# Scale and shift of the second layer's experts summed in chunks on VectorE, ScalarE and GpSimd, with the partitions added by TensorE

## The chip, the cores and the metric

One core of a Trainium2 chip. The metric is device time of one execution in microseconds (us), the median over runs; the profile is of one execution. TensorE is the matrix engine, VectorE (DVE), ScalarE (ACT) and GpSimd (POOL) the elementwise engines, SyncE (SP) issues most DMA loads. Each engine takes its instructions in a fixed order and waits on semaphores for what others produce.

## The reference, cut to what matters

A two-layer backbone over 256 latent tokens with 256 context tokens, width 1024, float32. Every sub-layer is modulated: a conditioning vector is multiplied by a 1024 x 6144 matrix per layer, which gives six vectors of 1024: shift, scale and gate of the mixer, shift, scale and gate of the expert layer.

```python
s_lat = jax.nn.silu(c)            # conditioning of the latents
s_ctx = jax.nn.silu(c_ctx)        # conditioning of the context
for layer in range(DEPTH):
    m  = [z[:, None, :] for z in ada_mod(s_lat, ada_w[layer], ada_b[layer])]
    mc = ada_mod(s_ctx, ada_w[layer], ada_b[layer])
    ...
    h = h + m[2] * y                                       # y: the mixer
    f = modulate(rmsnorm(h, norm_ffn_g[layer]), m[3], m[4])
    ...
```

`ada_mod` is `s @ w + b` split in six, `modulate(h, shift, scale)` is `h * (1 + scale) + shift`. In the second (last) layer the context no longer passes through the experts, so there `m[3]` and `m[4]` are needed for the latents only. The second layer's mixer is pooling in four groups beside windowed attention with eight heads of queries, then the output projection `odd_w_out`; the experts are 16 with two chosen per token.

## The kernel before, in words

The kernel runs the layers as phases in one program; in each, a scheduler lays the instructions of every engine into one fixed order. All weights pass as 1-MB tiles of shape [128, 4, 512] through `Stream`, a ring of seven buffers that SyncE fills (L147): a tile's buffer takes the next load when its last reader is done. For the projections, `Stream._prep` splits a half tile into two pieces, `whi` by a ScalarE copy (L176) and `wlo` by a subtraction on VectorE or, every third, on GpSimd (L180).

The modulation is made by `ada(l, i, half)` for half a vector (512 columns): two tiles, eight chunks [128, 512], and for each chunk a matmul (L446) of 32 columns of the conditioning `sT` with the chunk as moving operand, into one of four strips of 32 partitions of a PSUM bank. The strips hold latents and context of up to eight half vectors. `finish` copies the bank to the SBUF tile `part` on ScalarE (L476), adds the partitions with four matmuls on the 0/1 matrix `sel` (L482) and adds the bias on VectorE into `mcol` (L484); `gain` (L472) turns a scale into (1 + scale) times the norm's weight. `finish` puts its second part into `pend`, which `flush` runs later. `part` has two buffers.

The change lies in the second layer's mixer phase, from some 635 to 735 us. It loops over eight attention units (two blocks of queries, four pairs of heads). `scores` makes the scores of a unit on TensorE (L1499), masks them and takes the maximum on VectorE (L1503, L1504), forms the negative maximum `nm` (L1507, L1508), the exponential with its sum on ScalarE (L1515), and normalises `p` on VectorE (L1519). `attend` transposes `p` on TensorE (L1532), copies it to `pTT` on VectorE and ScalarE (L1534) and multiplies by the values (L1539). The scores of the next unit are requested ahead of the products of this one. In the first four rounds a pooling group is done as well (L1479 to L1486, split in L523, L524) and one half vector of modulation, `ada(*next(ada_it))`: the four half vectors of shift and scale for the experts. They share one PSUM bank and have one `finish`. In round 4 `flush` ends them; the rows are written to DRAM and read back spread over the partitions (`rows`, `spread`: L494 to L500, tiles `mrow` and `s4b`). Rounds 4 and 5 hold the output projection (`mix`, products L518 to L520; L528 multiplies by the gate `m2b` into `am`, L529 adds to the stream `H`, on VectorE for one half and on GpSimd for the other). Round 6 and the end prepare the input of the experts, then comes the router and the expert layer, which is matmuls of TensorE against streamed weights to the end.

Of the kernel before, what the change touches and what calls it, by code (L numbers as in the profile page):

```python
# [10 lines left out]
F32 = mybir.dt.float32  # L11
F32R = mybir.dt.float32r
I32 = mybir.dt.int32
AF = mybir.ActivationFunctionType
OP = mybir.AluOpType
# [51 lines left out]
UMAX = 6  # L67
# [145 lines left out]
def backbone(ctx: ExitStack, tc: tile.TileContext, I, out):  # L213
    nc = tc.nc
    V, S, G, T, Q = nc.vector, nc.scalar, nc.gpsimd, nc.tensor, nc.sync
# [3 lines left out]
    sm = ctx.enter_context(tc.tile_pool(name="sm", bufs=2))  # L219
# [13 lines left out]
    def tr_t():  # L233
        return psum.tile([128, 512], F32, name="tr", tag="tr", bufs=2)


    st = Stream(tc, ring, RING, NPIECE)
# [143 lines left out]
    one = cst[:, C_ONE:C_ONE + 128]  # L381
# [18 lines left out]
    c1 = cp.tile([128, 128], F32, name="c1")  # L400
# [18 lines left out]
    pend = []  # L419
    marks = {}  # L420

    def flush():
        while pend:
            pend.pop(0)()
# [11 lines left out]
    def ada(l, i, half, bank=y_t):  # L436

        g, u = group[l, i, half]
        first, last = (l, i, half) == g[0], (l, i, half) == g[-1]
        if first:  # L440
            mods[g] = bank()
        pa = mods[g]
        for s in range(2):
            t = st.take(("ada", l, i, half))
            for j in range(4):
                T.matmul(pa[32 * j:32 * j + 32, :], s_at(s * 4 + j, u), t[:, j, :],  # L446
                         start=first and s == 0, stop=last and s == 1, skip_group_check=True)
            st.done()
        if last:
            l, i, half = min(g)  # L450
            k0 = i * 8 + half * 4
            finish(l, mods.pop(g), len(g), 4, lambda t: t[:, k0:k0 + 4 * len(g)].rearrange("p (u q) c -> p u q c", q=4))
            for i in (1, 4):
                if (l, i, 0) in g:
                    pend.append(lambda i=i: gain(l, i, 0, 8))

    def ada_quarter(q):
        pa = y_t()
# [10 lines left out]
    def gain(l, i, k, n):  # L469
        m = mcol[l][:, i * 8 + k:i * 8 + k + n]  # L470
        gc = c1[:, 96 + 8 * l:104 + 8 * l] if i == 1 else c2[:, 8 * l:8 * l + 8]
        V.scalar_tensor_tensor(m, m, 1.0, gc[:, k:k + n, None].to_broadcast([128, n, 2]), op0=OP.add, op1=OP.mult)  # L472
# [878 lines left out]
    with phase("odd") as op:  # L1351
# [226 lines left out]
        for n, u in enumerate(units):  # L1578
            if n + 1 < len(units):
                scores(*units[n + 1])  # L1580
            if n < 4:
                f = pool_group(n)
            attend(*u)
            if n < 4:
                f()
            if n < 6 - NPRE:
                ada(*next(ada_it))
            if n == 4:
                flush()
                rows(1, 3, 5, 1)  # L1590
                t = op.tile([128, 2, D], F32, name="s4b", tag="band")
                sb["s4"], sb["b3"] = t[:, 0], t[:, 1]
                spread(t[:, 0], 1, 4, 0)
                spread(t[:, 1], 1, 3, 0)
                rws, lgb = router_setup(1, op, 1, rw)
            if n in (4, 5):
                w = st.take(("oo", n - 4))
                for c in range(2):
                    mix(0, c, n - 4, w)
                st.half()  # L1600
                st.done()
            if n == 5:
                ws = [st.take(("ooa", half)) for half in range(2)]
                io = st.taken - 2
                for half in range(2):
                    mix(1, 0, half, ws[half])
            if n == 6:
                ffn_in(0)
                for p in ADA_ODD[6:]:
                    ada(*p, mm_t)  # L1610
# [266 lines left out]
```

## Time and profile before

| | |
|---|---|
| median of 3 runs | 987.55 us (985.78 to 989.07) |
| profiled execution | 986.68 us |
| its span | 984.9 us, mean granted clock of TensorE 0.968 |
| GpSimd busy | 324.9 us |
| ScalarE busy | 313.6 us |
| moved by DMA | 296.27 MB |

The span runs from the first to the last instruction, and the 1.8 us between it and the execution's time lie around it. Busy times are of the engine's own instructions, waits not counted. In a timeline, a row is a run of like instructions on one engine: start, length, line, output and inputs, how many, and in brackets how long the engine stood idle before and which instruction ended that. A matmul in float32 appears as two records, so the four matmuls of L482 read x8.

### The profile page before, as it was taken

What the parts mean: (1) busy time and instruction counts of PE and PEld (TensorE: products, weight loads), DVE (VectorE), ACT (ScalarE), POOL (GpSimd) and SP (SyncE); (2) the same over time, 40 slices, a digit from 0 to 9 for tenths busy, and PEclk for the clock granted to TensorE, in tenths of its full rate; (3) what the DMA queues carried; (4) which work ended last, traced back from release to release, by engine and by line L of the source; (5) the groups of instructions that cost most, each with busy time, mean ns of one, the idle gap of its engine ahead of it and who ended that gap; (6) DMA issues with size and microseconds to landing.
All of it is one profiled execution on the core that took longest, in us unless ns stands there. A gap on an engine that the chain in (4) does not pass through costs nothing. (4 is left out here: it accounts for less than half of the span.)

```text
span 984.9 us, 12562 instructions
## 1 busy us (share of the span) xinstructions
PE 911.3 (93%) x4614; PEld 562.6 (57%) x4614; DVE 501.5 (51%) x903; ACT 313.6 (32%) x460; POOL 324.9 (33%) x231
## 2 busy tenths in 40 slices
PE   3999999988899999999999978898969999999984
PEld 1677667755684668656855647646554444443321
DVE  3562435276783668557774578356652133232222
ACT  3421113033473347226552444244311010010001
POOL 2351103334553465724660544113200022222222
PEclk9999999998899999999999989989979899999998
DMA  9974569848779879789979976259798999999993
GB/s 314 362 259 163 214 216 338 325 142 293 280 267 364 311 268 378 277 322 367 319 262 388 377 248 224 78 150 312 253 368 338 360 371 416 388 362 418 415 396 132
DMA packets 118867, 296.27 MB, mean 301 GB/s; under 512 B 6920, under 2 KB 17176, under 8 KB 110600
## 3 DMA queue, kind: packets, MB, share of 16 engines
q1 hardware_dynamic: 112776, 278.06, 77.2%
q0 software_dynamic: 5984, 17.26, 4.9%
q8 instruction: 40, 0.66, 0.3%
q14 instruction: 35, 0.29, 0.1%
q10 hardware_dynamic: 32, 0.01, 0.0%
HBM read 295.45 MB, written 4.24 MB: 304 GB/s over the span
## 5 line engine op out<-in xcount | busy, mean ns | idle before, releaser
L176 ACT ACTIVATE whi<-w 128x1024 fp32r<-128x1024 f32 x162 | 169.9, 1058 | 183.8 <-PE mm L520 83.3
L180 POOL TENSOR_TENSOR wlo<-w,whi 128x1024 fp32r<-128x1024 f32 x57 | 146.0, 2563 | 224.6 <-ACT whi L176 186.9
L180 DVE TENSOR_TENSOR wlo<-w,whi 128x1024 fp32r<-128x1024 f32 x105 | 157.4, 1512 | 81.8 <-ACT whi L176 81.3
L934 PE MATMUL mm<-w,xh 128*64 128x512 f32 (+2 forms) x680 | 171.4, 602 | 1.2 <-DMA w<-in_moe_w_up_dram 1.2
L529 POOL TENSOR_TENSOR H<-H,am 128x512 f32<-128x512 f32 x64 | 88.8, 1405 | 174.3 <-DVE am L528 171.9
L934 PEld LDWEIGHTS mm<-w,xh 128*64 128x64 f32 (+2 forms) x680 | 53.3, 138 | 94.3 <-issue 87.8
L518 PE MATMUL mm<-whi,xh 128*128 128x512 f32 x160 | 65.9, 412 | 0.8 <-ACT xh L523 0.8
L519 PE MATMUL mm<-wlo,xh 128*128 128x512 f32 x160 | 65.2, 407 | 0.3 <-POOL wlo L180 0.3
L520 PE MATMUL mm<-whi,xl 128*128 128x512 f32 x160 | 64.9, 406 | 0.0
L528 DVE TENSOR_TENSOR am<-mm,m5b 128x512 f32<-128x512 f32 x64 | 42.9, 684 | 27.9 <-PE mm L1262 19.5
L1262 PE MATMUL mm<-y,seT 128*128 128x512 f32 x208 | 54.5, 397 | 0.2 <-ACT y L523 0.2
L519 PE MATMUL mm<-aTl,whi 128*128 128x512 f32 x128 | 51.6, 403 | 2.0 <-POOL aTl L680 2.0
L518 PE MATMUL mm<-aTh,whi 128*128 128x512 f32 x128 | 51.4, 407 | 1.0 <-ACT aTh L679 1.0
L520 PE MATMUL mm<-aTh,wlo 128*128 128x512 f32 x128 | 51.1, 400 | 0.0
L1262 PEld LDWEIGHTS mm<-y,seT 128*128 128x128 f32 x208 | 38.1, 188 | 15.5 <-issue 4.9
L968 PE MATMUL yp<-w,hh 128*64 128x512 f32 (+1 forms) x176 | 42.8, 596 | 0.0
L524 DVE TENSOR_TENSOR yl<-yp,yh 128x512 fp32r<-128x512 f32 x14 | 9.7, 692 | 61.4 <-ACT yh L523 61.4
L446 PE MATMUL yp<-w,sT 128*32 128x512 f32 x288 | 40.8, 625 | 0.0
L934 PE MATMUL yp<-w,hh 128*64 128x512 f32 (+1 forms) x160 | 34.4, 643 | 5.5 <-SPq L1131 3.5
L1053 ACT ACTIVATE sg<-mm 128x512 f32<-128x512 f32 x21 | 12.4, 589 | 82.6 <-PE mm L934 77.1
L518 PEld LDWEIGHTS mm<-whi,xh 128*128 128x128 f32 x160 | 31.2, 195 | 10.9 <-issue 2.7
L1054 DVE SCALAR_TENSOR_TENSOR sg<-sg,slw,mm 128x512 f32<-128x512 f32 x21 | 15.6, 742 | 42.8 <-PE mm L934 42.8
(358 smaller groups left out, 1531.1 us busy)
## 6 DMA issues: line engine op xcount, KB each, us to landing
w<-in_moe_w_gate_dram SPq DMA_DIRECT2D x54, 1024.0 KB
w<-in_moe_w_down_dram SPq DMA_DIRECT2D x54, 1024.0 KB
w<-in_moe_w_up_dram SPq DMA_DIRECT2D x50, 1024.0 KB
w<-in_ada_w_dram SPq DMA_DIRECT2D x48, 1024.0 KB
w<-in_even_w_in_dram SPq DMA_DIRECT2D x8, 1024.0 KB
w<-in_moe_w_gate_dram SPq DMA_DIRECT2D x16, 512.0 KB
w<-in_moe_w_up_dram SPq DMA_DIRECT2D x16, 512.0 KB
w<-in_moe_w_down_dram SPq DMA_DIRECT2D x12, 512.0 KB
```

Source lines behind the costliest of these rows:

```text
L176: self.nc.scalar.activation(hi, t, AF.Copy)
L180: eng.tensor_sub(lo, t, hi.bitcast(F32))
L446: T.matmul(pa[32 * j:32 * j + 32, :], s_at(s * 4 + j, u), t[:, j, :], start=first and s == 0, stop=last and s == 1, skip_group_check=True)
L518: T.matmul(o, lh, rh, start=first, stop=False)
L519: T.matmul(o, lh, rl, start=False, stop=False)
L520: T.matmul(o, ll, rh, start=False, stop=last)
L528: V.tensor_mul(t, pp, m)
L529: eng.tensor_add(acc, acc, t)
L934: T.matmul(o[hs], xh[:, kk, hs].bitcast(F32), w[h][:, k], start=first and k == 0, stop=last and k == 3, skip_group_check=True)
L968: T.matmul(o[hs], hh[:, j, hs].bitcast(F32), w[h][:, k], start=j == 0, stop=j == 3, skip_group_check=True)
L1054: V.scalar_tensor_tensor(sg, sg, w, pu, op0=OP.mult, op1=OP.mult)
L1262: marks["comb"] = T.matmul(pp, seT[n][:, c * 128:(c + 1) * 128], t[:, hs], start=(i == 0), stop=(i == 2 * len(ns) - 1))
```

## The change

For the four half vectors, `ada` is replaced by `ada_sum`, which leaves out the context. It does not multiply on TensorE. The chunk's 128 rows are scaled by the conditioning, one value per partition, and the eight chunks of a half vector are added into two [128, 512] accumulators. Odd chunks go to VectorE: a scaled copy, then three multiply-adds. Even chunks go to ScalarE, a scaled copy into the accumulator, then three scaled copies into a tile `as` that GpSimd adds. The second part, `fin`, adds the 128 partitions: eight matmuls with a 128x128 piece of an accumulator as the weights and a column of ones as the moving operand. Then come the bias and, after the last, the gain. Every `ada_sum` begins with `flush`, so it first emits the `fin` of the one before. The accumulators are the two buffers of `part`; `as` is one of the three buffers `t2k`. Lines of the changed kernel from L489 on are 33 higher than before.

```diff
--- before.py
+++ after.py
@@ -453,6 +453,39 @@
             for i in (1, 4):
                 if (l, i, 0) in g:
                     pend.append(lambda i=i: gain(l, i, 0, 8))
+
+    def ada_sum(l, i, half, tmp):
+
+        flush()
+        accs = [sm.tile([128, 512], F32, name="part", tag="part", bufs=2) for _ in range(2)]
+        for s in range(2):
+            t = st.take(("ada", l, i, half))
+            for j in range(4):
+                a, x = accs[j % 2], sT[:, s * 4 + j, 2 * UMAX - 2:2 * UMAX - 1]
+                if s == 0 and j == 1:
+                    V.tensor_scalar(a, t[:, j, :], x, None, op0=OP.mult)
+                elif j % 2:
+                    V.scalar_tensor_tensor(a, t[:, j, :], x, a, op0=OP.mult, op1=OP.add)
+                elif s == 0 and j == 0:
+                    S.activation(a, t[:, j, :], AF.Copy, scale=x)
+                else:
+                    y = tmp("as")
+                    S.activation(y, t[:, j, :], AF.Copy, scale=x)
+                    G.tensor_add(a, a, y)
+            st.done()
+        k0 = i * 8 + half * 4
+
+        def fin():
+            pc = tr_t()
+            for q in range(4):
+                for n, a in enumerate(accs):
+                    T.matmul(pc[:, q:q + 1], a[:, q * 128:(q + 1) * 128], one[:, 0:1], start=(n == 0), stop=(n == 1))
+            V.tensor_add(mcol[l][:, k0:k0 + 4, 0], pc[:, 0:4], c1[:, 48 * l + k0:48 * l + k0 + 4])
+            if half and i == 4:
+                m = mcol[l][:, i * 8:i * 8 + 8, 0]
+                V.scalar_tensor_tensor(m, m, 1.0, c2[:, 8 * l:8 * l + 8], op0=OP.add, op1=OP.mult)
+
+        pend.append(fin)
 
     def ada_quarter(q):
         pa = y_t()
@@ -1584,7 +1617,7 @@
             if n < 4:
                 f()
             if n < 6 - NPRE:
-                ada(*next(ada_it))
+                ada_sum(*next(ada_it), t2k)
             if n == 4:
                 flush()
                 rows(1, 3, 5, 1)
```

Where the order changes, three places. First VectorE at the start of attention: before, from the copy `U` of the input projection to the negative maximum `nm` of the first unit (`mm` are the scores, `mx` the maxima).

```order
L1473 COPY U<-mm 128x512
L1503 TENSOR_TENSOR mm<-mm,mask 128x128
L1504 TENSOR_REDUCE mx<-mm 128x1
L1503 TENSOR_TENSOR mm<-mm,mask 128x128
L1504 TENSOR_REDUCE mx<-mm 128x1
L1503 TENSOR_TENSOR mm<-mm,mask 128x128
L1507 SCALAR_TENSOR_TENSOR nm<-mx,snk 128x2
L1504 TENSOR_REDUCE mx<-mm 128x1
L1508 TENSOR_SCALAR nm<-nm 128x2
```

The same place in the changed kernel, to the same `nm`:

```order
L1506 COPY U<-mm 128x512
L1536 TENSOR_TENSOR mm<-mm,mask 128x128
L1537 TENSOR_REDUCE mx<-mm 128x1
L1536 TENSOR_TENSOR mm<-mm,mask 128x128
L517 TENSOR_TENSOR mcol_137<-tr,c_122 128x8
L466 TENSOR_SCALAR part<-w,sT 128x512
L1537 TENSOR_REDUCE mx<-mm 128x1
L468 SCALAR_TENSOR_TENSOR part<-w,sT,part 128x512
L1536 TENSOR_TENSOR mm<-mm,mask 128x128
L1540 SCALAR_TENSOR_TENSOR nm<-mx,snk 128x2
L1536 TENSOR_TENSOR mm<-mm,mask 128x128
L468 SCALAR_TENSOR_TENSOR part<-w,sT,part 128x512
```

The scaled copy and two multiply-adds of the first sum now stand ahead of the second part of that `nm` (which follows after one more reduction).

Second SyncE, around the loads of the output projection's weights (`wa` and `wb` are halves of an expert weight, `m2b` the gate). Before:

```order
L140 DMA wa<-in_moe_w_up_dram 128x1024
L497 DMA mrow_139<-rowt 8x128
L500 DMA m2b<-mrow_139 128x1024
L147 DMA w<-in_odd_w_out_dram 128x4x512
L147 DMA w<-in_odd_w_out_dram 64x4x512 x2
L147 DMA w<-in_odd_w_out_dram 128x4x512
L147 DMA w<-in_odd_w_out_dram 64x4x512 x2
L147 DMA w<-in_ada_w_dram 128x4x512 x4
```

In the changed kernel:

```order
L140 DMA wa<-in_moe_w_up_dram 128x1024
L147 DMA w<-in_odd_w_out_dram 128x4x512
L530 DMA mrow_139<-rowt 8x128
L147 DMA w<-in_odd_w_out_dram 64x4x512 x2
L533 DMA m2b<-mrow_139 128x1024
L147 DMA w<-in_odd_w_out_dram 128x4x512
L147 DMA w<-in_odd_w_out_dram 64x4x512 x2
L147 DMA w<-in_ada_w_dram 128x4x512 x3
```

The first output weights moved ahead of the row's write to DRAM and of the gate's load.

Third VectorE around the third and fourth unit's `pTT`. Before, from the `es` of a unit to the output projection's `am`:

```order
L1511 TENSOR_TENSOR es<-snk,nm 128x2
L1486 TENSOR_SCALAR pT<-tr,c_122 128x256
L1534 COPY pTT<-tr 128x512
L1486 TENSOR_SCALAR pT<-tr,c_122 128x256
L1534 COPY pTT<-tr 128x512
L524 TENSOR_TENSOR ml_5584<-yp,mh_5583 128x4x128
L528 TENSOR_TENSOR am<-mm,m2b 128x512
```

In the changed kernel, from the bias of the second sum on (L483 is the bias of a sum):

```order
L483 TENSOR_TENSOR mcol_137<-tr,c_122 128x4
L466 TENSOR_SCALAR part<-w,sT 128x512
L468 SCALAR_TENSOR_TENSOR part<-w,sT,part 128x512 x3
L1567 COPY pTT<-tr 128x512
L1519 TENSOR_SCALAR pT<-tr,c_122 128x256
L557 TENSOR_TENSOR ml_5584<-yp,mh_5583 128x4x128
L483 TENSOR_TENSOR mcol_137<-tr,c_122 128x4
L466 TENSOR_SCALAR part<-w,sT 128x512
```

The whole third sum of VectorE stands ahead of that `pTT` copy, behind the bias of the second, and the fourth sum begins behind the bias of the third.

## Rows read from the trace of the kernel before

**Rows 1.** The page, its first part: busy time of each engine, share, instructions
```profile
PE 911.3 (93%) x4614; PEld 562.6 (57%) x4614; DVE 501.5 (51%) x903; ACT 313.6 (32%) x460; POOL 324.9 (33%) x231
```

**Rows 2.** Lines by form, 634 to 730 us: busy us, mean ns, idle before
```profile
L446 PE MATMUL yp<-w,sT 128*32 128x512 f32 x64 | 8.4, 603 | 0.0
```

**Rows 3.** TensorE's timeline: start, length, line, count, [idle before <-releaser]
```profile
641.46 4.45 PE L1499 MATMUL mm<-kT,qT 64*128 64x512 f32 x8 [1.62 <-ACT p L1515]
645.84 1.97 PE L1532 MATMUL tr<-idt,p 128*128 128x128 f32 x8
...
661.01 1.92 PE L446 MATMUL yp<-w,sT 128*32 128x512 f32 x16
...
663.93 1.09 PE L1539 MATMUL yp<-pTT,vv 128*64 128x128 f32 x14
...
668.59 0.50 PE L518 MATMUL mm<-whi,mh 128*128 128x512 f32 x1 [2.07 <-ACT p L1515]
...
674.24 1.09 PE L1539 MATMUL yp<-pTT,vv 128*64 128x128 f32 x14 [0.79 <-ACT pTT L1534]
...
678.58 0.43 PE L1539 MATMUL yp<-pTT,vv 128*64 128x128 f32 x2
...
679.57 1.09 PE L1539 MATMUL yp<-pTT,vv 128*64 128x128 f32 x14
680.59 1.09 PE L1532 MATMUL tr<-idt,p 128*128 128x128 f32 x8
...
683.37 1.06 PE L482 MATMUL tr<-csm,part 128*128 128x8 f32 x8
684.36 1.13 PE L1499 MATMUL mm<-kT,qT 64*128 64x512 f32 x4
...
686.43 0.50 PE L518 MATMUL mm<-whi,mh 128*128 128x512 f32 x1
```

**Rows 4.** ScalarE's timeline, 636 to 700 us
```profile
639.33 1.28 ACT L1515 ACT_TABLE_LOAD   x1 [2.57 <-DVE nm L1508]
...
665.56 2.00 ACT L176 ACTIVATE whi<-w 128x1024 fp32r<-128x1024 f32 x2 [4.79 <-DMA w<-in_odd_w_out_dram]
```

**Rows 5.** VectorE's timeline, 634 to 700 us
```profile
684.57 2.04 DVE L1519 TENSOR_SCALAR p<-p,den 128x512 f32<-128x512 f32 x2
...
694.45 0.68 DVE L528 TENSOR_TENSOR am<-mm,m2b 128x512 f32<-128x512 f32 x1
```

**Rows 6.** GpSimd's timeline, 560 to 700 us
```profile
683.65 2.68 POOL L529 TENSOR_TENSOR H<-H,am 128x512 f32<-128x512 f32 x2 [2.15 <-DVE den L1516]
...
694.01 2.78 POOL L180 TENSOR_TENSOR wlo<-w,whi 128x1024 fp32r<-128x1024 f32 x1 [1.75 <-ACT whi L176]
```

**Rows 7.** Lines by form, whole span, three instructions of the sums' shapes
```profile
L476 ACT ACTIVATE part<-yp 128x512 f32<-128x512 f32 x6 | 3.5, 592 | 10.3 <-PE yp L446 10.3
...
L843 DVE SCALAR_TENSOR_TENSOR mixT<-z,c,mixT 128x512 f32<-128x512 f32 x4 | 3.0, 743 | 0.0
...
L1420 POOL TENSOR_TENSOR qr<-t,t 128x512 f32<-128x512 f32 x2 | 2.6, 1291 | 1.1 <-DVE t L1418 1.1
```

**Rows 8.** VectorE's timeline, 115 to 129 us
```profile
116.19 0.48 DVE L842 TENSOR_SCALAR mixT<-z,c 128x512 f32<-128x512 f32 x1
...
120.22 2.58 DVE L842 TENSOR_SCALAR mixT<-z,c 128x512 f32<-128x512 f32 x1
```

**Rows 9.** GpSimd's timeline, 115 to 129 us
```profile
119.76 2.76 POOL L180 TENSOR_TENSOR wlo<-w,whi 128x1024 fp32r<-128x1024 f32 x1 [15.14 <-ACT whi L176]
```

**Rows 10.** SyncE's timeline: when loads are issued
```profile
650.73 7.31 SPq L147 DMA_DIRECT2D w<-in_odd_w_out_dram  x6
```

**Rows 11.** 4-us windows: busy us by engine, granted clock, DMA share, GB/s
```profile
644.00:648.00 4.00, 4.00 (x13) 2.17 (x12) 3.02 (x10) 0.16 (x1) 0.00 (x0) 0.50 0.00 0
```

**Rows 12.** Waits of TensorE, 735 to 985 us: total us, times, longest
```profile
PE yp L934 <- SPq L1131: 3.5, 3, 1.7
```

**Rows 13.** Waits of SyncE, 640 to 985 us
```profile
SPq L147 <- PE mm L934: 66.1, 19, 15.1
```
## Prediction

> **What bounds the kernel now.** The page comes first: TensorE is busy 911.3 us, 93% of the span of 984.9, VectorE 51% [rows 1]. The reader is to see that a gain must come from TensorE's queue, either as work taken out of it or as waits. Second, the waits by line: after the stage that is changed, from 735 us to the end, TensorE's largest entry is 3.5 us [rows 12], while SyncE's loads wait 66.1 us for TensorE to free their buffers [rows 13]. The weights are there before they are wanted, so a shift of TensorE in the stage from 634 to 735 us passes on to the end almost one to one. Third, the lines by form of that stage give what is taken out: 64 records, 8.4 us [rows 2]. Fourth, TensorE's timeline, to see where those records lie and what it waits for: they lie among the scores and products of the first attention units, the last of them at 661.01, and of its waits two are over a microsecond, 1.62 and 2.07, both for the exponential [rows 3].
>
> **The change part by part.** I go along TensorE's queue and carry its shift against before at five marks: the ends of the second, third and fourth unit (665.0, 675.3 and 680.7, each the start of a row plus its length), the first product of the second output half at 686.43, and the end of the stage [rows 3].
>
> *TensorE's own work.* The four products with the weights leave: -8.4 [rows 2]. The one partition sum over the strips, eight records in 1.06 us at 683.37, leaves too [rows 3]. In its place stand four sums with ones, each eight matmuls of one column. Before, four matmuls made the eight records, so a sum has sixteen; the time is that of loading 128x128 weights rather than of columns, so I price a record as there at 1.06/8 = 0.13 us: 2.1 us a sum, 8.4 in all. TensorE's work changes by -8.4 - 1.06 + 8.4 = -1.1 us. It is hardly relieved; what decides is where the others stand when it asks.
>
> *What the others get.* A sum costs VectorE one scaled copy, 0.48 [rows 8], and three multiply-adds of 0.743, the same form as L843 [rows 7]: 2.7 us. ScalarE makes four copies of 0.59, 2.4 us, and GpSimd three additions of 1.29, 3.9 us [rows 7]. That is 10.8, 9.5 and 15.5 us for the four; all three have the room as a share, so only the place counts.
>
> *First sum.* VectorE's order puts the scaled copy and two multiply-adds ahead of `nm`, the input of the first exponential: 0.48 + 2 x 0.743 = 1.96. The exponential's table load starts at 639.33 as soon as `nm` is there [rows 4], and TensorE already waits for it. So +1.9. All 64 old records lie ahead of the second unit's end, and one sum with ones comes there: -8.4 + 1.9 + 2.1 = **-4.4**.
>
> *Loads.* SyncE issues the first output weights in front of the `mrow` and `m2b` loads instead of behind them, and their buffer now comes free with the first sum (VectorE, ScalarE and GpSimd have read it near 640 us) instead of at 650.73 [rows 10]. ScalarE waited 4.79 us for the second tile and TensorE 2.07 us behind it [rows 3, 4]. That goes: -2.07. The three other loads passed are small or issue early, and cost nothing, because TensorE has these weights ahead of need. What is late next is the second sum: both of its accumulators are the two buffers that the first sum's matmuls must have read.
>
> *Second sum.* One scaled copy and one multiply-add (1.2 us) stand before the first `pTT` copy of the third unit, which TensorE needs, and the matmuls with ones add 2.1. At the third unit's end: -4.4 - 2.07 + 1.2 + 2.1 = **-3.2**.
>
> *Third sum.* VectorE runs it whole, scaled copy and three multiply-adds, between the second sum's finish and the `pTT` copy of the fourth unit. TensorE holds 3.3 us of other work there (from the third unit's end at 675.3 to the fourth's first product at 678.58 [rows 3]). Freely, VectorE needs 0.48 + 2.2 and, as `am` from PSUM to SBUF, 0.68 for the copy [rows 5]: 3.4 us, a wait of 0.1. But GpSimd's three additions become ready at that moment. No row of before has a multiply-add from SBUF under a GpSimd instruction, so I bound it. The nearest rows: a scaled copy of 0.48 took 2.58 when GpSimd's 2.76 us subtraction was under way [rows 8, 9], and a pair of scaled copies 2.04 beside two additions of GpSimd, to the end of the second [rows 5, 6]. An operation that reads PSUM, `am` at 694.45, kept its 0.68 within a GpSimd subtraction of 2.78 [rows 5, 6]. If each multiply-add first sits out an addition, the three take 3 x (1.29 + 0.74) = 6.1, with the two copies 7.3, and TensorE waits 4.0. I take the held price, as the rows nearest to it (operands in SBUF on both sides) are all held. Fourth unit's end: -3.2 + 4.0 = **+0.8** (free: -3.1).
>
> The Trainium skill, "SBUF — State Buffer", section "Who interferes with whom", says that VectorE and GpSimd share one pair of SBUF ports as an exclusive lock for a whole instruction, and that a VectorE instruction with two SBUF inputs contends with a GpSimd instruction that reads SBUF. By that rule the third sum costs the upper value, and every addition moved to GpSimd speaks against this change; the trace agrees with the lock on other forms (2.58 against 0.48), and no run here shows it for the multiply-add.
>
> *Fourth sum and the end.* The third sum's ones, less the old partition sum: 2.1 - 1.06 = +1.0. The fourth sum's multiply-adds stand around the next normalisation of `p`, two of them ahead of it. Freely they hide under TensorE's transposes and output products; held under additions of 1.29 they cost up to 2.3. I take half, 1.1, since the operations that TensorE asks for there (`pTT`, `am`) read PSUM, which wasn't held. The last sum's ones: +2.1. So at the end: 0.8 + 1.0 + 1.1 + 2.1 = **+5.0** us, with bounds 0.0 (nothing held: -3.1 + 1.0 + 2.1) and +6.2 (all held).
>
> The sum is made against the profiled execution, 986.68 us for a span of 984.9: 991.7. The median of the three runs lies 0.87 above that execution, so on the median's footing it is 992.6; I give 992.2, between the two.
>
> **The rivals.** One: *no difference*. VectorE isn't held, GpSimd gives way, or its additions come at other moments: the lower bound, +0.0, so 987.5 by the median. For it: the shift of -4.4 at the second unit is certain arithmetic, and no more than 5.0 us of held time is at stake (4.0 - 0.1 + 1.1). A second way to the same time, that the weight stream swallows the shift later, has TensorE's 3.5 us of waits for loads against SyncE's 66.1 for TensorE against it [rows 12, 13]. Chance 0.30 in all.
>
> Two: *faster*, by the clock. After its 1.62 us wait TensorE's granted clock is 0.50 from 644 to 648 us, the lower of its two levels (1.2 GHz of 2.4) [rows 11]. The eight score records take 4.45 there where four take 1.13 at full clock, and eight transposes 1.97 instead of 1.09: 2.2 + 0.9 = 3.1 us [rows 3]. If nothing is held and TensorE gets through this stretch at full clock, the end is 0.0 - 3.1, and the 0.8 us wait at 674.24 may go as well: -3.9, so 983.6. It decides at 641 us: TensorE must have work there, or a shorter wait. The order speaks against, since that wait becomes longer by 1.9. Chance 0.15.
>
> Three: *slower still*. The longer first wait, or the 4.0 us in the third sum, brings the clock down for another such stretch: 5.0 + 3.1 = +8.1, so 995.7 by the median; with everything held, +9.3, 996.9. For it: a 1.62 us stop came just ahead of the drop. Against: the 2.07 us stop at 668 left the fourteen products of a unit at the same 1.09 us as before it, at 674.24 and at 663.93 [rows 3]. Chance 0.13.
>
> **How the numbers follow.** About 0.3%, 3.0 us, is what a measurement of this kernel can tell from no change: 984.6 to 990.5. The forecast, held in the third sum, has 0.42, all slower; with the third rival 0.55 for slower, 0.30 for no difference, 0.15 for faster. The range goes from the fast rival's 983.5 to 998.0, a microsecond over the held bound with the clock's price; it leaves out half of the fast rival and some of the slow one. The forecast's own range is 990 to 994.5.
>
> **What would show it.** Right: the first exponential near 641.2; no wait on the output weights on ScalarE; the second unit ending near 660.6; multiply-adds of 2 us instead of 0.74 beside GpSimd's additions, and a TensorE wait of 3 to 4 us on the VectorE's `pTT` near 674; sixteen records of 0.13 us per sum. Wrong: multiply-adds at 0.74 throughout, or records with one column far from 0.13, or a first wait that didn't grow. If GpSimd's additions are long over when the multiply-adds start, the third sum's step fails and the time falls to 987.5.

## The result and the profile after

The change makes the kernel slower: median 999.92 us (995.57 to 1007.26, six runs) against 988.55 us (985.78 to 989.92), ratio 1.0115 with a 95% interval of 1.009 to 1.014, which is 11.4 us. The forecast of slower held. Its 992.2 us was too low, and the result lies outside the range of 983.5 to 998.0. The profiled execution took 1000.71 us for a span of 999.0, so it is 14 us over the profiled one of before, a little more than the medians say. The first part of its page, for [rows 1]:

```profile
PE 921.5 (92%) x4606; PEld 574.8 (58%) x4606; DVE 521.5 (52%) x922; ACT 323.7 (32%) x475; POOL 341.9 (34%) x243
```

TensorE's busy time grew by 10 us (911.3 before) though the change leaves it less to do. TensorE's timeline shows where. Columns as in [rows 3]; scores are L1532, transposes L1565, products with the values L1572, sums with ones L482, the output projection L551 to L553.

```profile
642.60 2.61 PE L1532 MATMUL mm<-kT,qT 64*128 64x512 f32 x4 [2.98 <-ACT p L1548]
...
655.94 1.12 PE L1532 MATMUL mm<-kT,qT 64*128 64x512 f32 x2
656.99 1.95 PE L482 MATMUL tr<-cst,part 128*128 128x1 f32 x16
658.87 1.12 PE L1532 MATMUL mm<-kT,qT 64*128 64x512 f32 x2
659.92 1.44 PE L1572 MATMUL yp<-pTT,vv 128*64 128x128 f32 x14
...
669.12 1.09 PE L1572 MATMUL yp<-pTT,vv 128*64 128x128 f32 x14 [0.77 <-ACT pTT L1567]
670.13 1.95 PE L482 MATMUL tr<-cst,part 128*128 128x1 f32 x16
...
678.61 0.69 PE L1572 MATMUL yp<-pTT,vv 128*64 128x128 f32 x2 [2.83 <-DVE pTT L1567]
...
680.38 1.97 PE L1572 MATMUL yp<-pTT,vv 128*64 128x128 f32 x14
682.28 3.58 PE L482 MATMUL tr<-cst,part 128*128 128x1 f32 x16
...
687.04 0.63 PE L552 MATMUL mm<-wlo,mh 128*128 128x512 f32 x1
...
696.25 0.80 PE L551 MATMUL mm<-whi,mh 128*128 128x512 f32 x1
...
699.97 1.84 PE L482 MATMUL tr<-cst,part 128*128 128x1 f32 x16
```

At my marks and at the fourth unit's first product, against [rows 3]: the second unit ends at 661.36 instead of 665.02 (-3.7), the third at 670.21 instead of 675.33 (-5.1), the fourth unit's first product starts at 678.61 instead of 678.58 (0.0), its last ends at 682.35 instead of 680.66 (+1.7). Then comes a break: the second output half starts at 696.25 instead of 686.43 (+9.8). The router's first matmul, long after the sums, is 13.3 us late (745.22 against 731.96).

From 678.61 on the same instructions take twice as long: fourteen products 1.97 instead of 1.09, sixteen records with ones 3.58 instead of 1.95, an output product 0.63 instead of 0.39. The 4-us windows (columns as in [rows 11]) say why: TensorE's granted clock is 0.50, the lower of its two levels (1.2 GHz), until the middle of the last window shown. In [rows 3] the same work ran at full clock.

```profile
676.00:680.00 4.00, 1.39 (x4) 0.79 (x4) 2.52 (x3) 1.69 (x3) 1.41 (x1) 0.70 0.94 357
...
680.00:684.00 4.00, 4.00 (x24) 3.29 (x23) 1.18 (x2) 2.03 (x5) 0.72 (x1) 0.50 0.78 291
684.00:688.00 4.00, 4.00 (x17) 3.71 (x18) 2.11 (x4) 1.05 (x3) 1.59 (x2) 0.50 0.00 0
688.00:692.00 4.00, 4.00 (x10) 1.75 (x8) 4.00 (x7) 1.06 (x1) 2.57 (x2) 0.50 0.35 78
692.00:696.00 4.00, 4.00 (x20) 2.09 (x19) 4.00 (x5) 0.59 (x1) 1.27 (x1) 0.50 0.59 207
696.00:700.00 4.00, 4.00 (x17) 3.03 (x14) 1.62 (x4) 0.00 (x0) 1.28 (x1) 0.74 0.96 371
```

Just there, from 675.78 to 678.61, TensorE stood still for 2.83 us, for `pTT`; the window from 676 to 680 has the clock at 0.70. What it waited for is in the others' timelines. VectorE, with the third sum's multiply-adds and the copy behind them:

```profile
672.88 5.08 DVE L468 SCALAR_TENSOR_TENSOR part<-w,sT,part 128x512 f32<-128x512 f32 x3
677.88 0.68 DVE L1567 COPY pTT<-tr 128x512 f32<-128x512 f32 x1
```

GpSimd, with the additions of the same sum:

```profile
672.76 4.65 POOL L474 TENSOR_TENSOR part<-part,as 128x512 f32<-128x512 f32 x3 [1.06 <-ACT part L470]
```

ScalarE, with a scaled copy of the fourth sum and the other `pTT`:

```profile
677.44 0.72 ACT L473 ACTIVATE as<-w,sT 128x512 f32<-128x512 f32 x1 [0.95 <-POOL part L474]
678.07 0.57 ACT L1567 COPY pTT<-tr 128x512 f32<-128x512 f32 x1
```

The third sum's three multiply-adds took 5.08 us, 1.69 each against 0.743 in [rows 7], while GpSimd made its three additions in 4.65. VectorE's copy of `pTT` came behind them, at 677.88. ScalarE's came at 678.07: it stood behind scaled copies that waited for the same additions, because the three buffers of `as` were full. The two copies, for two different reasons, were equally late.

### The profile page after: what moved, and what is told of

Same layout as the page of the kernel before. It is cut to its first block, busy times and chain, and to the rows that moved or that the text cites. A ratio compares the mean times of both kernels' runs of the same rounds, so it can differ in the third digit from the quotient of the medians.

```text
span 999.0 us, 12606 instructions
## 1 busy us (share of the span) xinstructions
PE 921.5 (92%) x4606; PEld 574.8 (58%) x4606; DVE 521.5 (52%) x922; ACT 323.7 (32%) x475; POOL 341.9 (34%) x243
## 5 line engine op out<-in xcount | busy, mean ns | idle before, releaser
L551 PE MATMUL mm<-whi,xh 128*128 128x512 f32 x160 | 66.1, 413 | 0.8 <-ACT xh L556 0.8
L553 PE MATMUL mm<-whi,xl 128*128 128x512 f32 x160 | 64.9, 405 | 0.0
L551 PE MATMUL mm<-aTh,whi 128*128 128x512 f32 x128 | 52.4, 415 | 1.0 <-ACT aTh L712 1.0
L553 PE MATMUL mm<-aTh,wlo 128*128 128x512 f32 x128 | 51.1, 400 | 0.0
L551 PEld LDWEIGHTS mm<-whi,xh 128*128 128x128 f32 x160 | 31.2, 195 | 11.0 <-issue 2.7
L552 PEld LDWEIGHTS mm<-wlo,xh 128*128 128x128 f32 x160 | 31.2, 195 | 8.8 <-issue 1.6
```

The lines of the kernel that those rows point to most:

```text
L551: T.matmul(o, lh, rh, start=first, stop=False)
L552: T.matmul(o, lh, rl, start=False, stop=False)
L553: T.matmul(o, ll, rh, start=False, stop=last)
```

## The experiments

Theory A: the third sum makes TensorE stand still, and it is the low clock behind that standstill that costs most. Theory B: the matmuls of one column bring the clock down. C: VectorE is too full. D: all engines together are too busy for the high clock. Changes below are against the changed kernel where nothing else is said, and "over" is against the kernel before.

### GpSimd's additions given to VectorE

```diff
...
-                    S.activation(y, t[:, j, :], AF.Copy, scale=x)
-                    G.tensor_add(a, a, y)
+                    V.scalar_tensor_tensor(a, t[:, j, :], x, a, op0=OP.mult, op1=OP.add)
...
```

> The additions leave GpSimd: the even chunks after the first are multiply-adds on VectorE too (six of 0.74 us and one copy per sum, 5.0 us in place of 2.7), two accumulators and eight matmuls with ones as before. Theory A (GpSimd's additions hold the multiply-adds, the 2.8 us stop of TensorE that follows brings the granted clock to 0.50 from 679 to 697 us, and that stretch is most of the loss): multiply-adds at 0.74 throughout, the wait for pTT about 1 us in place of 2.8, no long stretch at 0.50, and 1 to 5 us over the kernel before, against 11 for the change. Theory B (the clock falls because of the matmuls of one column, whatever VectorE does): the low stretch stays, 10 to 13 us over. Theory C (VectorE is simply too full): 14 us over or more, as it gets 9 us of work more.

Ratio 1.0084 (1.0051 to 1.0117), some 8 us over, between the cases of A and B. The stretch at 0.50 from 679 is gone, and the wait for `pTT` there is 0.92 us. But TensorE now stands still ahead of the first softmax, as its timeline shows:

```profile
648.77 3.78 PE L1528 MATMUL mm<-kT,qT 64*128 64x512 f32 x6 [8.55 <-ACT p L1544]
```

VectorE's timeline tells what came late. The input `nm` of that softmax stands behind a split of the output weights, and ScalarE, which makes the first half of the split, had waited 4.95 us for their load. Then `nm`, two columns wide, took 2.30 us itself, beside a subtraction of GpSimd of 2.43 us that began at 643.25:

```profile
642.26 1.22 DVE L180 TENSOR_TENSOR wlo<-w,whi 128x1024 fp32r<-128x1024 f32 x1 [3.41 <-ACT whi L176]
643.40 2.30 DVE L1536 SCALAR_TENSOR_TENSOR nm<-mx,snk 128x2 f32<-128x2 f32 x1
```

The 4-us windows have the low clock behind the stop, and further down a short dip:

```profile
648.00:652.00 4.00, 3.23 (x6) 1.61 (x6) 2.33 (x9) 2.91 (x10) 0.00 (x0) 0.50 0.82 296
...
680.00:684.00 4.00, 4.00 (x16) 3.13 (x14) 2.89 (x5) 0.37 (x1) 0.00 (x0) 0.57 0.94 326
```

So the stop moved and the low clock moved with it. My expected time was wrong: I had looked at the third sum alone. The same four groups of one-column matmuls are in this kernel, and behind the one at 677.35 the clock was low for one window only; that speaks against B as the cause of the long stretch. Most of the loss stays, but not because VectorE is too full, as C has it: ahead of this stop VectorE had stood still for 3.41 us itself.

### Half the matmuls with ones

```diff
+        V.tensor_add(accs[1], accs[1], accs[0])
...
-                for n, a in enumerate(accs):
-                    T.matmul(pc[:, q:q + 1], a[:, q * 128:(q + 1) * 128], one[:, 0:1], start=(n == 0), stop=(n == 1))
+                T.matmul(pc[:, q:q + 1], accs[1][:, q * 128:(q + 1) * 128], one[:, 0:1], start=True, stop=True)
```

> VectorE adds the two accumulators into one (0.68 us a sum more), and the matmuls with ones are four instead of eight, 1.0 us a sum instead of 2.0. Theory A: the hold by GpSimd and the stop of TensorE stay or grow by 0.7, the clock still falls to 0.50 in the fourth unit; the 4 us saved at full clock show, so 6 to 9 us over the kernel before. Theory B: half the matmuls with ones, half the loss or less: 3 to 5 us over, and a shorter stretch at 0.50. Theory C: 12 us over.

Ratio 1.0104 (1.0078 to 1.013), as slow as the change although TensorE has 4 us less to do. That contradicts B, which asked for half the loss; it is also a little above A's 6 to 9 us. The waits of TensorE in the stage tell what took the saving: 7.0 us for `pTT` on VectorE in three waits, 4.0 for `am`, 3.0 for the first exponential, 2.0 for `pT`.

### The old products kept as well

```diff
+        pa = y_t()
...
+            for j in range(4):
+                T.matmul(pa[32 * j:32 * j + 32, :], s_at(s * 4 + j, 0), t[:, j, :], start=s == 0, stop=s == 1,
+                         skip_group_check=True)
```

> As the change, but TensorE also makes the old products of the same eight chunks with 32 columns of the conditioning (64 records, 8.4 us in all), whose result nobody reads. It asks what the clock hangs on. Theory A (the clock falls after TensorE stood still): these products fill TensorE's queue in the softmax units, the wait for pTT shrinks below 1 us and the clock stays high; 8.4 us of work more and some 8 us of low clock less, so 8 to 13 us over the kernel before, about as the change. If instead the clock falls because all engines together are too busy (theory D), it falls the same or longer and the time is 18 us over or more.

Ratio 1.0179 (1.0151 to 1.0207), 18 us over: at the edge where I had put theory D. But the products didn't fill the wait. The scheduler moved them elsewhere, TensorE stood still for 4.8 us on `pTT` near 680 and the clock was 0.50 behind it again. As a test of D the run is inconclusive.

### VectorE alone, one accumulator

```diff
-        accs = [sm.tile([128, 512], F32, name="part", tag="part", bufs=2) for _ in range(2)]
+        accs = [sm.tile([128, 512], F32, name="part", tag="part", bufs=2) for _ in range(1)]
-                a, x = accs[j % 2], sT[:, s * 4 + j, 2 * UMAX - 2:2 * UMAX - 1]
+                a, x = accs[0], sT[:, s * 4 + j, 2 * UMAX - 2:2 * UMAX - 1]
...
-                    S.activation(y, t[:, j, :], AF.Copy, scale=x)
-                    G.tensor_add(a, a, y)
+                    V.scalar_tensor_tensor(a, t[:, j, :], x, a, op0=OP.mult, op1=OP.add)
...
```

> The whole sum on VectorE alone: one accumulator, one scaled copy and seven multiply-adds (5.7 us), four matmuls with ones (1.0 us). A sum takes only one of the two buffers, so the next need not wait for the matmuls of the last; the first two sums then stand ahead of the first softmax in VectorE's order. TensorE's own work is 8.4 + 1.1 - 4.2 = 5.3 us less than before. Theory A: no hold, the first exponential no later than before, one stop of about 1 us by the third sum: between 5 us under the kernel before and 2 over. Theory B: half of the one-column matmuls: 3 to 6 us over. Theory C: 10 us over or more.

Ratio 1.0064 (1.0032 to 1.0095), above my 2 us. TensorE's work is 5 us less than in the kernel before, and yet it loses 6. VectorE runs the second sum ahead of the first softmax (one multiply-add of it took 2.85 us beside a subtraction of GpSimd), TensorE waits 6.4 us for the first exponential, and the clock is 0.50 in the windows from 648 to 660 us.

### VectorE's accumulator in PSUM

```diff
+        pb = y_t()
...
-                a, x = accs[j % 2], sT[:, s * 4 + j, 2 * UMAX - 2:2 * UMAX - 1]
+                a, x = (accs[0], pb)[j % 2], sT[:, s * 4 + j, 2 * UMAX - 2:2 * UMAX - 1]
...
+        S.activation(accs[1], pb, AF.Copy)
```

> VectorE's accumulator lies in PSUM instead of SBUF, so that a multiply-add reads one operand from SBUF and one from PSUM; ScalarE copies it to SBUF at the end (0.6 us a sum). GpSimd's additions, the eight matmuls with ones and the place of the multiply-adds ahead of pTT stay. Theory A (GpSimd's hold on VectorE, then TensorE's stop, then the clock): the multiply-adds are no longer held, 0.74 in place of 1.7 in the third sum; the wait for pTT falls from 2.8 below 1 us; no long stretch at 0.50 from 679; 2 to 5 us over the kernel before, since the first softmax is still 1.4 us later. Theory B (the one-column matmuls bring the clock down): 10 to 13 us over, as the change. Theory C (VectorE too full): 8 to 11 us over, since VectorE's queue only loses the hold.

Ratio 1.0094 (1.0069 to 1.012). The hold is gone: a multiply-add within GpSimd's additions keeps its 0.74 us. VectorE's timeline, one of them:

```profile
661.51 0.74 DVE L469 SCALAR_TENSOR_TENSOR yp<-w,sT,yp 128x512 f32<-128x512 f32 x1
```

GpSimd's, the additions around it:

```profile
658.45 4.14 POOL L475 TENSOR_TENSOR part<-part,as 128x512 f32<-128x512 f32 x3
```

The Trainium skill, "SBUF — State Buffer", section "Who interferes with whom", has it so: a VectorE instruction with at most one SBUF input, outside the two-port modes, doesn't contend with GpSimd. This trace agrees (0.74 here, 1.69 in the change with both inputs in SBUF).

The time did not follow: some 9 us over is a miss for A's 2 to 5 and within C's 8 to 11. But the stop that took the place of this one isn't VectorE's. The weights of the output projection came late, ScalarE waited 2.44 us for them with its `pTT` copy queued behind, and TensorE stood still for 3.59 us. The clock is 0.50 behind it. ScalarE's timeline:

```profile
669.90 1.06 ACT L176 ACTIVATE whi<-w 128x1024 fp32r<-128x1024 f32 x1 [2.44 <-DMA w<-in_odd_w_out_dram]
670.86 0.57 ACT L1569 COPY pTT<-tr 128x512 f32<-128x512 f32 x1
```

TensorE's, the stop and the fourteen products behind it at the low clock:

```profile
671.48 1.97 PE L1574 MATMUL yp<-pTT,vv 128*64 128x128 f32 x14 [3.59 <-ACT pTT L1569]
```

### The matmuls with ones by themselves

This one is the kernel before, with nothing summed.

```diff
                 ada(*next(ada_it))
+                pc = tr_t()
+                for q in range(4):
+                    for e in range(2):
+                        T.matmul(pc[:, q:q + 1], idt, one[:, 0:1], start=(e == 0), stop=(e == 1))
```

> The kernel before, with four more groups of eight one-column matmuls (on the identity, result unused), one in each of the first four rounds, and nothing else. It prices the matmuls with ones and their effect on the clock by themselves. Theory A: four times 1.95 us of TensorE's queue, a short dip of the granted clock behind one of them at most: 6 to 9 us over the kernel before. Theory B: the long stretch at 0.50 appears here too: 14 us over or more. If they hide in TensorE's waits: 2 to 5 over.

Ratio 1.0072 (1.0042 to 1.0102), 7 us over, as theory A had it. The lines by form give the price:

```profile
L1591 PE MATMUL tr<-cst,idt 128*128 128x1 f32 x64 | 7.8, 251 | 0.0
```

The windows give the clock:

```profile
668.00:672.00 4.00, 4.00 (x25) 3.48 (x22) 3.58 (x11) 1.84 (x8) 0.73 (x1) 0.77 1.04 354
672.00:676.00 4.00, 4.00 (x19) 3.20 (x19) 0.03 (x1) 0.76 (x2) 0.00 (x0) 0.81 1.04 385
676.00:680.00 4.00, 3.65 (x34) 2.74 (x32) 1.15 (x2) 1.54 (x3) 3.04 (x2) 1.00 1.06 402
```

64 records take 7.8 us, against the 8.4 that I had summed. The clock dips to 0.77 and 0.81 for two windows and is back: no long stretch. These matmuls by themselves bring no long stretch at 0.50, which B asked for; a short dip can come with them.

### Two sums of the four

```diff
...
-                ada_sum(*next(ada_it), t2k)
+                p = next(ada_it)
+                ada_sum(*p, t2k) if p[1] == 3 else ada(*p)
```

In the second run it is `== 4`; the pair that is not summed is a group of its own for `ada`.

> Only the two halves of the shift (first two rounds) are summed; the two of the scale are made as before, with their own finish. TensorE's own work is about the same as before (4.2 and 0 us less, 3.9 more). The second sum runs whole ahead of a pTT copy on VectorE, beside GpSimd's additions. Theory A: the first softmax 1.4 us later; one hold of some 2 to 3 us, and if TensorE stands still for it, a low stretch: 4 to 9 us over. If the old products in rounds 3 and 4 fill the hold: 0 to 3 over. Theory B: half of the matmuls with ones: 5 to 6 over.

> Only the two halves of the scale (rounds three and four) are summed; the two of the shift are made as before, with their own finish. The first softmax has no sum in it, so its wait stays 1.6 us. Theory A: the hold in the first of the two sums stays (two multiply-adds and GpSimd's additions ahead of a pTT copy), TensorE waits 2 us or so and the clock falls in the fourth unit: 6 to 10 us over. If the wait there is below 1 us: 0 to 3 over and no low stretch. Theory B: 5 to 6 over whatever the wait is.

The first two halves alone: 1.0056 (1.0029 to 1.0084). The last two alone: 1.0018 (0.9994 to 1.0043), no difference that can be told. The first keeps the 3.0 us wait of the first softmax, with the clock at 0.50 from 644 to 648, and has a 2.2 us wait for `pTT`. The second has one wait of 2.8 us and one window at 0.50 (664 to 668). The first pair costs about half of the whole. The last pair is a miss for theory A, which had 6 to 10 us: its stop is as long as that of the change (2.80 us, for `pTT`), but by the windows from 660 us (0.75, 0.50, 0.89) the clock is low for some 7 us only, under twelve output products, and little is lost. A stop alone doesn't fix the price.

### Work in the standstill

The decisive one. Ten matmuls, whose result the products overwrite, stand exactly where TensorE waited for `pTT`; no other instruction of the stage changes its place in its engine's order.

```diff
...
+            if (b, c) == (0, 3):
+                with tc.issue_after(last.ins):
+                    for e in range(10):
+                        T.matmul(ob[b][:, c * 128:(c + 1) * 128], idt, qT[:, 0, 0:128], start=True, stop=True, skip_group_check=True)
```

> The change with every engine's order as it is, and ten matmuls of 128 columns more on TensorE (idle work, overwritten by the products that follow) between the transposes of the fourth unit and its first product: just where TensorE stood still for 2.8 us. Ten such matmuls take 2.7 us at full clock, as the eight transposes' records take 1.09. Theory A (the standstill brings the granted clock down): TensorE works through the wait, the clock stays at 1.00 from 679 to 697 us, and the time falls by 7 to 9 us against the change, to 2 to 5 us over the kernel before, although there is more work. Theory B (the matmuls with ones do it) or D (all engines too busy): the low stretch stays, 11 to 14 us over.

Ratio 1.0039 (1.0023 to 1.0055): 3.9 us over in place of 11.4. TensorE's timeline, from the idle matmuls (L1572) on:

```profile
675.74 2.40 PE L1572 MATMUL yp<-qT,idt 128*128 128x128 f32 x20
678.75 0.43 PE L1576 MATMUL yp<-pTT,vv 128*64 128x128 f32 x2 [0.61 <-DVE pTT L1567]
...
679.74 1.09 PE L1576 MATMUL yp<-pTT,vv 128*64 128x128 f32 x14
680.76 1.95 PE L482 MATMUL tr<-cst,part 128*128 128x1 f32 x16
...
689.55 0.50 PE L551 MATMUL mm<-whi,mh 128*128 128x512 f32 x1 [1.24 <-DVE am L561]
```

Its windows:

```profile
676.00:680.00 4.00, 3.39 (x28) 2.69 (x28) 2.71 (x4) 1.81 (x3) 1.54 (x1) 1.00 0.97 350
...
680.00:684.00 4.00, 4.00 (x39) 3.66 (x36) 2.38 (x7) 2.94 (x7) 1.17 (x2) 1.00 0.81 302
684.00:688.00 4.00, 4.00 (x25) 1.95 (x25) 4.00 (x4) 1.64 (x2) 3.84 (x3) 1.00 0.36 90
688.00:692.00 4.00, 2.76 (x17) 2.08 (x14) 4.00 (x6) 0.00 (x0) 1.51 (x2) 1.00 0.41 172
692.00:696.00 4.00, 4.00 (x27) 3.59 (x26) 3.97 (x8) 0.00 (x0) 2.04 (x2) 1.00 0.88 295
```

VectorE, ScalarE and GpSimd are as late as before (the first product starts at 678.75, in the change at 678.61), but the clock stays at 1.00 through all five windows and the second output half starts at 689.55 instead of 696.25. More work on TensorE, and 7.5 us less time (1.0115 less 1.0039 of 988). That is theory A shown: the late `pTT` is in both kernels, the low clock behind it only in the change, and it costs some 7 us. Theory B goes with it, since the four groups with ones are in both kernels, and theory D, since the other engines do the same work here at full clock. Theory C can explain why `pTT` is late, which it still is here, and not the 7 us.

### Both waits for pTT eased

The accumulator is in PSUM as above, and besides:

```diff
...
+                    with ExitStack() as q:
+                        if (i, half) == (4, 1):
+                            q.enter_context(tc.issue_after(marks["pTT"].ins))
+                        S.activation(y, t[:, j, :], AF.Copy, scale=x)
```

> The accumulator in PSUM as in the run with that change alone, and besides the scaled copies of the fourth sum on ScalarE stand behind the pTT copies of the fourth unit instead of ahead of them, so that neither pTT copy waits for GpSimd's additions. Theory A: where the accumulator alone left a stop of 3.6 us on ScalarE's pTT, no stop over 1.2 us is left near 668 us and no long low stretch; 3 to 6 us over the kernel before (the ones cost 7.8 and save 9.5, the waits of about 1 us each remain). If another wait takes its place (the fourth sum's own end, or the ones): 7 to 10 over with a stop above 2 us to be seen there. Theory B: 10 us over with no stop above 1.2 us.

Ratio 1.0081 (1.0052 to 1.0111), a miss for A's 3 to 6 us: ScalarE's `pTT` was again behind a split of the output weights that hadn't arrived (2.69 us), TensorE waited 3.7 us and the clock fell. That is the second of the expectation's cases, another wait in the place of the first, and its 7 to 10 us. Which of the two paths to `pTT` would decide alone in the change stays open: both edits with the accumulator in PSUM let the weights' load come last.

### One sum, in the input projection

On VectorE alone with one accumulator, as above; the other three half vectors form one group of `ada`.

```diff
+                p = next(ada_it)
+                ada_sum(*p, t2k) if n == 0 else ada(*p)
...
```

> Only the first half vector is summed, on VectorE alone with one accumulator, and its eight operations stand in the input projection, where VectorE has idle time; the other three go the old way in one bank. TensorE: sixteen records (2.1 us) less, four matmuls with ones (1.0 us) more, the old partition sum stays: 1.1 us less. Theory A: no new stop, so no low clock beyond that of the kernel before: 1 to 3 us under it, a difference at the edge of what can be measured. Theory B: a short dip of the clock behind the one group with ones, 0 to 2 us over.

Ratio 1.0042 (1.0025 to 1.006): a miss, slower where I had hoped for less time, and above B's case too. TensorE's waits in the projection tell a part: 2.4 us in one wait for `wlo`, which VectorE subtracts and which now stands behind operations of the sum (1.55 in the kernel before), and the clock is 0.64 in the window behind it, where it was 1.00 before. VectorE's time in the projection was not free. The rest of the 4 us is not accounted for.

### The standstills of the kernel before

Sixteen idle matmuls in the kernel before, in the 4.51 us wait for `oh` ahead of the positions; in the second run seven more in the first softmax.

```diff
...
+        if nch == 2:
+            with tc.issue_after(marks["rows"].ins):
+                for e in range(16):
+                    T.matmul(pp[:, 256:384], idt, idt, start=True, stop=True, skip_group_check=True)
```

> The kernel before, with sixteen idle matmuls of 128 columns (some 4.3 us at full clock, result unused) on TensorE just where it stands still for 4.51 us ahead of the router's positions (727.4 to 732 us); every other instruction keeps its place. In the profile of before the granted clock is 0.50 behind that standstill until some 742 us, and 32 records take 7.88 us there. Theory A (a standstill of TensorE brings the clock down, in this kernel everywhere): the clock stays at 1.00, the 32 records take some 4.4 us, and the time falls by 3 to 5 us under the kernel before. Theory B (what lowers the clock in the change is its one-column matmuls, and this stretch has another cause, such as the 4- and 16-column matmuls there): no difference, 0 to 1 us over.

> As the run before it, and seven more idle matmuls in the first softmax, where TensorE of the kernel before stands still for 1.62 us and the clock is 0.50 from 644 to 648 us; the scheduler moves old modulation products up behind them. Theory A: that stretch goes too (3.1 us by its rows), 6 to 8 us under the kernel before. Theory B: 0 to 2 us over. If the moved products delay the second unit by more than the clock gives: 2 to 5 us under, as the run before it.

The first: ratio 0.9979 (0.9960 to 0.9998), 2 us under the kernel before, and so the fastest kernel of this study, if by less than a measurement of one change can be sure of. TensorE's timeline, from the idle matmuls (L594) on:

```profile
728.46 3.74 PE L594 MATMUL tr<-idt 128*128 128x128 f32 x32
...
736.41 7.88 PE L1693 MATMUL tr<-sgm,f 128*128 128x128 f32 x32 [0.28 <-DVE slw L1670]
```

Its windows:

```profile
732.00:736.00 4.00, 1.92 (x14) 1.60 (x13) 3.63 (x24) 0.00 (x0) 0.00 (x0) 1.00 0.98 362
736.00:740.00 4.00, 3.72 (x17) 3.66 (x17) 1.35 (x8) 0.00 (x0) 0.00 (x0) 0.57 1.01 424
...
740.00:744.00 4.00, 4.00 (x19) 4.00 (x19) 0.00 (x0) 0.59 (x1) 0.00 (x0) 1.00 1.00 417
```

In the kernel before these three are at 0.50, 0.50 and 0.76. The direction is theory A's. My 3 to 5 us were too much: the 32 records of L1693 take the same 7.88 us with the clock as it is here and as it was before, so they are not paced by it.

The second: 1.0073 (1.0046 to 1.01), 7 us over where every case had less time, in a kernel without any sum. The filled wait let the clock stay at 1.00 to 660 us, but the old products moved up, and VectorE's `pT` stood behind a split of the output weights, for which VectorE itself had waited 3.48 us. TensorE waited anew:

```profile
664.12 1.12 PE L1540 MATMUL tr<-idt,p 128*128 128x128 f32 x4 [3.28 <-DVE pT L1494]
```

Behind that wait the clock is at 0.50 for four windows:

```profile
664.00:668.00 4.00, 3.88 (x9) 1.81 (x10) 2.79 (x8) 3.85 (x11) 1.19 (x1) 0.50 1.03 314
668.00:672.00 4.00, 4.00 (x9) 1.84 (x10) 2.35 (x9) 0.58 (x1) 0.00 (x0) 0.50 1.05 388
672.00:676.00 4.00, 4.00 (x16) 1.85 (x16) 3.00 (x9) 1.61 (x4) 0.84 (x1) 0.50 1.07 400
676.00:680.00 4.00, 4.00 (x16) 3.11 (x13) 0.42 (x1) 0.72 (x4) 0.00 (x0) 0.50 1.01 411
```

So the price belongs to the standstill and the work behind it, and needs neither the sums nor their matmuls with ones.

## Why the prediction was wrong in size

**TensorE's own work**: right. -8.4 and -1.06 leave, and the ones were 1.95 a group at full clock (3.58 for the third at the low one) against the 2.1 forecast: 7.8 for 8.4 in the run that has nothing else. TensorE is not relieved.

**First sum**: right in kind, smaller. TensorE's wait is 2.98 instead of 1.62 and the scores start at 642.60 instead of 641.46, so +1.1 where I had +1.9: ScalarE loaded its table ahead of the wait this time. Even so the second unit ended only 3.7 us early (forecast 4.4). The sum lacked two things. Four records of scores, 1.13 us in one row before (684.36 in [rows 3]), were split by the ones into two rows of two, which took 1.12 each (655.94 and 658.87): +1.1. And the clock dipped behind the ones, so that the fourteen products took 1.44 instead of 1.09.

**Loads**: right. The 2.07 us wait at 668.59 is gone, ScalarE's longest wait for the weights is 1.43 us for 4.79.

**Second sum**: its ones came just behind my mark instead of ahead of it, so the third unit ended 5.1 us early where I had 3.2.

**Third sum**: right. The multiply-adds were held (1.69 each for 2.0 forecast), TensorE waited 2.83 us for 4.0, and the fourth unit began at the time of before, as the sum had it within a microsecond. I had named the hold as the only cause; ScalarE's copies behind the `as` buffers were a second one, just as late.

**Fourth sum and the end**: right. Its three multiply-adds were held too, 1.37, 1.64 and 1.78 us in the change, 2.6 more than free, where my bound was 2.3. With the clock kept up by the idle matmuls the second output half starts 3.1 us late (689.55 against 686.43), where the sum had 0.8 + 1.0 + 1.1 = 2.9; the last ones took 1.84 for 2.1.

**The step that failed** is the price of a wait. The sum charged the 4.0 us in the third sum by their length, with TensorE's work behind them at full clock, and left the clock to the third rival, "slower still": that a stop brings it down "for another such stretch", priced at 3.1 us from one stretch of the kernel before, with a chance of 0.13. It came, and was larger than the rival had it. By the windows the clock was low for some 20 us (0.70, four times 0.50, 0.74), where the stretch of the kernel before has some 7 (0.87, 0.50 and 0.78 from 640 us), and the price was 6.7 us (696.25 less 689.55, with and without work in the stop) to 7.5 (by the two ratios, whose intervals leave some 3 us to either side). I had even the reason against it from one row, that the 2.07 us stop at 668 was followed by no fall, and made too much of it. And I passed over a row that speaks for it: that only two waits are over a microsecond is true of the attention units alone. TensorE of the kernel before also stands still for 4.51 us ahead of 731.96, with the clock at 0.50 in the two windows behind it.

With the clock kept up, the change is 3.9 us over, and the sum had said 5.0. That these are so near is in part luck: the first wait and the hold cost 0.8 and 1.2 us less than in the sum, and the split scores and the dip behind the first ones, which it lacked, cost about as much more.

**The same, and the faster rival**: the wait for the first exponential grew, so the clock did not stay up at 641 us, and nothing was swallowed by the weight stream: the 13.3 us at the router are 14 at the end of the span.

## What to carry to other kernels

Price a new wait of the engine that bounds the kernel not by its length alone but by the clock of the work behind it, and look in the windows of the trace for the granted clock after each standstill that the kernel already has. Moving work off a full engine pays only if what it then waits for is earlier than before: here TensorE gave up 9.5 us of matmuls and got 7.8 back as others, and stood still for the rest. Where a standstill can't be removed, some idle matmuls in it are an experiment of four lines that tells the two prices apart, and may be a gain, or, where they move other work, a loss, as in the last run.

## What the runs showed that was not expected

- How long the clock stays low behind a standstill differs widely. The stops of 2.83 us in the change and of 3.28 in the last run went with some 20 and 17 us of low clock by the windows, the second without any matmul with ones; a stop of 2.80 us (with the last two sums alone) with some 7; a stop of 4.04 us (with half the ones) with one window at 0.57, behind which TensorE made output products without a gap; the 2.07 us of the kernel before with none. What sets the length is not shown: the idle matmuls show only that, with work in the stop, the stretch doesn't come.
- The granted clock fell also where TensorE had not stood still: to 0.57 from 660 to 664 us in the change, behind the first group with ones at 656.99. In the kernel before with the ones alone, 0.77 and 0.81 for two windows. It was not always so: behind the second group, at 670.13, the clock stayed at 1.00.
- GpSimd holds small instructions too. In the change `den`, two columns wide, took 1.22 us at 660.59 beside the additions of the second sum, and `es` 2.18 at 668.86 beside a subtraction of 2.35, where either takes 0.15 elsewhere. The sum priced the hold for the multiply-adds alone.
- In four runs (no additions on GpSimd, both with the accumulator in PSUM, and the last) the longest stop stood behind a split of the output weights whose load came late: with another order of the engines another wait comes last.
- A busy TensorE can be a slow TensorE: its busy time went up by 10 us, with 8 records fewer.
